# Reordering a convolution stage: three projection blocks ahead of the depthwise blocks, one joint LayerNorm tail, and squares and issues moved to GpSimd

**The chip, the cores, the metric.** The kernel runs on all 8 cores of one Trainium2 chip, each core with its own slice of the tokens. The metric is the device time of the slowest core in microseconds (us). Executions fall into two states: a fast one in which all cores show the same granted clock (the share of TensorE's full clock that the chip let through), and a slow one in which one die (or both) shows a lower clock and the time is some per cent longer, whatever the kernel. The five engines are called PE (TensorE, matmul), DVE (VectorE), ACT (ScalarE), POOL (GpSimd) and SP (SyncE, which here only starts transfers). In profile lines, `ps` is PSUM, the memory that PE writes its results to.

## The reference

Four layers, each a token mixer and a SwiGLU feed-forward network (FFN), each behind an RMS norm. Layers 1 and 3 use the mixer that this study is about:

```python
def conv_mixer(h, past, w_pw1, b_pw1, w_dw, b_dw, ln_g, ln_b, w_pw2, b_pw2):
    a = h @ w_pw1 + b_pw1                                   # pointwise-1: 1024 -> 2048
    glu = a[..., :D_MODEL] * jax.nn.sigmoid(a[..., D_MODEL:])
    padded = jnp.concatenate([past, glu], axis=1)
    new_state = padded[:, -CONV_STATE:]                     # last 30 rows, an output
    c = depthwise_conv(padded, w_dw, width=31) + b_dw       # one filter per channel
    c = jax.nn.silu(layer_norm(c, ln_g, ln_b))              # norm over the 1024 channels
    y = c @ w_pw2 + b_pw2                                   # pointwise-2: 1024 -> 1024
    return y, new_state
# in the trunk, per layer:  x = x + mixer(rms_norm(x));  x = x + swiglu(rms_norm(x))
```

## The kernel before

Channels lie on the 128 partitions, so 1024 channels are 8 blocks (`kc` 0 to 7). A core makes two passes over its tokens (`p` 0 and 1), with three token tiles in each (`tt`, widths 384, 384 and 256 in pass 0, up to 384, 384 and 320 in pass 1). A convolution stage therefore runs four times: two layers by two passes. I number them stages 1 to 4; 3 and 4 are pass 1.

A small scheduler records each operation with what it reads and writes and puts it on one engine's in-order queue; waits follow from the data. The depthwise convolution is done on PE: `stack` copies a pair of channel blocks four times, shifted, into a stacked buffer (16 transfers), and `dw` multiplies that with small 128x32 diagonal weights. The LayerNorm needs sums over channels, so a block's output is cast to bf16 and squared, and PE sums both with a matrix of ones.

```python
    def stat_a(kc, tt):                       # cast and square of one block, for the sums
        k_ = 2 * (len(slots) % 4)             # four shared slot pairs in SQ
        ...
        P.op("pool" if kc < 5 else "dve", ... tensor_copy(out=SQ[:, k_, 0:n], in_=CC.v[:, kc, c0:c0 + n]))
        P.op("act", ... activation(out=SQ[:, k_ + 1, 0:n], in_=CC.v[:, kc, c0:c0 + n], func=AF.Square))

    def stat_b(kc, tt): ...                   # PE adds both into two PSUM banks
    def ln_stats(tt): ...                     # mean and 1/std of one tile, in FT[0], FT[1]
    def ln_apply(tt):                         # scale 8 blocks, then 8 Silus, for one tile
        ...
                P.op("pool" if kc > 5 else "dve", ... tensor_tensor(CC, CC, FT[f], op))

    pw1(0); stack(0); build_w(0); build_w(1)
    pw1(1); stack(1)
    for kc in (0, 1):
        build_w(kc + 2)
        for tt in range(3): dw(kc, tt)
    pw1(2); stack(2)
    for kc in (2, 3):
        build_w(kc + 2)
        for tt in range(3): dw(kc, tt)
    pw1(3); stack(3, ("sp", "act"))
    load_p2(0); load_p2(1)                    # pointwise-2 weights, 1 MB each, on POOL's queue
    ...
    for tt in range(3):
        for kc in range(4): stat_a(kc, tt)
        dw(4, tt)
        for kc in range(4): stat_b(kc, tt)
    ...                                       # blocks 5 to 7 tile by tile, each tile's
    ...                                       # ln_stats and ln_apply between the next tile's blocks
    for tt in range(3):
        for m in range(KC):
            pw2(m, tt)                        # tile 2's statistics fall between these
            ...
                nnorm.square(k_, tt, *tb[tt]) # squares for the next RMS norm, on ACT
        nnorm.later(...)
```

## Time and profile before

| | kernel before |
|---|---|
| fast runs, all rounds of the study | 3903 to 3917 us, a few up to 3958 |
| profiled run (fast) | 3910.3 us, slowest core's span 3908.8 us |
| PE busy | 3633.7 us (93%) |
| span minus PE busy | 275 us, of which 156 us in the four convolution stages |
| table loads on ACT (instruction ACT_TABLE_LOAD) | 93 |

PE is the bound, so the profile is to be read for PE's idle time and for what ended it: the view of PE's waits gives the releaser, the timeline gives the place. Two readings are easily mixed up. A wait for a named tile ends when some engine or transfer has made it. A wait for "issue" is one in which nothing that the profile shows was missing.

### The profile page before, as it was taken

The page shows a single profiled execution, that of the slowest core. Times are in us where ns is not written, and L with a number is a line of the kernel's source. Part 1 is how long each engine was busy: PE and PEld are TensorE (multiplying, and loading weights), DVE is VectorE, ACT ScalarE, POOL GpSimd, SP SyncE. Part 2 cuts the span into 40 slices and gives each one's busy share as a digit, 9 for nine tenths or more (in the row PEclk, how much of TensorE's full clock was granted, in tenths as well). Part 3 has the DMA queues.
Part 4 walks back from the last instruction along what each step waited for, and adds up shares of the span by engine and source line. Part 5 has one row for each costly group of instructions (what it writes and reads, how often), then busy time and mean ns, then how long its engine had stood idle before and what let it go on. Part 6 is the DMA issues. An engine that isn't in the chain of part 4 may idle for free.

```text
span 3908.8 us, 71376 instructions; the slowest of 8 cores (3889.9 to 3908.8 us)
## 1 busy us (share of the span) xinstructions
PE 3633.7 (93%) x26325; PEld 2286.6 (59%) x26325; DVE 1710.2 (44%) x3324; ACT 1085.0 (28%) x2043; POOL 243.0 (6%) x376
## 2 busy tenths in 40 slices
PE   6999997899999999799599999879999999987998
PEld 2565664466466666466346666546664656654665
DVE  4875223521777213422377721334238772133422
ACT  3322112611432213521233211243124231124311
POOL 0000000100000000100001000020001000001000
PEclk9999998999999999899799999989999999998999
DMA  5443446244443445244534344544344434353433
GB/s 129 77 71 60 76 71 128 55 76 71 81 82 60 80 73 109 58 87 74 140 73 83 64 77 77 105 76 76 61 75 80 82 62 80 71 104 64 75 60 91
DMA packets 83807, 311.96 MB, mean 80 GB/s; under 512 B 14800, under 2 KB 27984, under 8 KB 66000
## 3 DMA queue, kind: packets, MB, share of 16 engines
q0 software_dynamic: 38016, 239.09, 34.8%
q1 hardware_dynamic: 42896, 63.75, 6.8%
q10 hardware_dynamic: 2560, 4.56, 0.6%
q8 instruction: 221, 3.62, 0.4%
q14 instruction: 114, 0.93, 0.1%
HBM read 499.23 MB, written 10.72 MB: 130 GB/s over the span
## 4 chain that ended last, share of the span: by engine, by line
PE 86%; DVE 4%; DMA 3%; issue 3%; ACT 2%; SPq 1%; ACTq 1%; DVEq 0%
PE ps L396 46%; PE ps L493 16%; PE ps L616 9%; PE ps L745 7%; PE ps L896 3%; PE ps L429 2%; DVE BIG L965 1%; SPq L880 1%; DMA xA<-xT 1%; DMA AUX<-BIG 1%; PE ps L701 1%; PE ps L391 1%; DVE xA L460 1%; ACTq L880 1%; DMA yT<-xA 1%
## 5 line engine op out<-in xcount | busy, mean ns | idle before, releaser
L396 PE MATMUL ps<-hA,RING 128*128 128x384 bf16 (+3 forms) x12672 | 1950.3, 314 | 2.7 <-issue 2.7
L396 PEld LDWEIGHTS ps<-hA,RING 128*128 128x128 bf16 x12672 | 1232.9, 98 | 640.9 <-issue 18.2
L485 DVE TENSOR_TENSOR BIG<-ps,FT 128x384 bf16<-128x384 f32 x528 | 276.1, 524 | 951.8 <-PE ps L396 906.9
L493 PE MATMUL ps<-BIG,RING 128*128 128x384 bf16 (+3 forms) x4224 | 634.0, 313 | 0.0
L493 PEld LDWEIGHTS ps<-BIG,RING 128*128 128x128 bf16 x4224 | 413.3, 98 | 217.4
L55 ACT ACTIVATE FT<-ps 128x384 f32<-128x384 f32 (+4 forms) x545 | 252.8, 465 | 968.9 <-PE ps L396 927.9
L460 DVE SCALAR_TENSOR_TENSOR xA<-ps,xA 128x384 f32<-128x384 f32 (+3 forms) x480 | 243.2, 522 | 567.4 <-PE ps L493 515.5
L55 ACT ACTIVATE SQ<-xA 128x384 bf16<-128x384 f32 (+3 forms) x432 | 188.9, 489 | 760.9 <-DVE xA L460 723.6
L745 PE MATMUL ps<-AUX,RING 128*128 128x384 bf16 (+3 forms) x2304 | 359.6, 312 | 21.6 <-DVE xA L460 21.2
L616 PE MATMUL ps<-RING,hA 128*128 128x512 bf16 x1584 | 345.3, 380 | 0.0
L745 PEld LDWEIGHTS ps<-AUX,RING 128*128 128x128 bf16 x2304 | 219.3, 98 | 140.0 <-issue 30.5
L616 PEld LDWEIGHTS ps<-RING,hA 128*128 128x128 bf16 x1584 | 155.2, 98 | 187.4 <-issue 2.2
L55 ACT ACTIVATE AUX<-ps,PPS 128x384 bf16<-128x384 f32 (+3 forms) x288 | 156.1, 557 | 362.8 <-PE ps L396 317.0
L445 DVE SCALAR_TENSOR_TENSOR hA<-xA,PPS,FT 128x384 bf16<-128x384 f32 (+3 forms) x384 | 194.3, 579 | 77.7 <-ACT FT L55 77.3
L713 DVE SCALAR_TENSOR_TENSOR FT<-ps,PPS,AUX 128x384 f32<-128x384 f32 (+1 forms) x288 | 163.7, 568 | 30.1 <-PE ps L701 23.0
L55 ACT ACTIVATE BIG<-ps 128x512 bf16<-128x512 f32 x198 | 118.1, 597 | 204.2 <-DVE ps L620 204.1
L729 DVE TENSOR_TENSOR AUX<-FT,AUX 128x384 bf16<-128x384 f32 (+3 forms) x288 | 151.3, 525 | 51.4 <-DVE FT L713 36.5
L620 DVE TENSOR_TENSOR ps<-ps,BV 128x512 f32<-128x512 f32 x210 | 145.9, 695 | 57.5 <-PE ps L616 55.8
L429 PE MATMUL ps<-SQ,ONESD 128*128 128x384 bf16 (+4 forms) x440 | 92.8, 326 | 83.8 <-ACT SQ L55 80.0
L832 DVE SCALAR_TENSOR_TENSOR BIG<-ps,PPS,FT 128x384 bf16<-128x384 f32 (+2 forms) x120 | 60.6, 508 | 235.2 <-PE ps L396 225.6
L53 ACT ACT_TABLE_LOAD x93 | 119.3, 1283 | 145.1 <-PE ps L429 41.6
L631 DVE BATCH_NORM_STATS2 STATS<-BIG 128x6 f32<-128x512 bf16 x198 | 135.4, 684 | 4.1 <-ACT BIG L55 3.9
(85 smaller groups left out, 1589.1 us busy)
## 6 DMA issues: line engine op xcount, KB each, us to landing
RING<-w_gu POOLq DMA_DIRECT2D x88, 1024.0 KB, 8.7
RING<-w_dn POOLq DMA_DIRECT2D x64, 704.0 KB, 6.6
RING<-w_v POOLq DMA_DIRECT2D x24, 1024.0 KB, 10.0
RING<-w_u POOLq DMA_DIRECT2D x32, 768.0 KB, 7.8
RING<-w_o POOLq DMA_DIRECT2D x32, 768.0 KB, 7.4
RING<-w_p POOLq DMA_DIRECT2D x24, 1024.0 KB, 10.5
AUX<-BIG SPq DMA_DIRECT2D x112, 147.0 KB, 8.5
AUX<-BIG SPq DMA_DIRECT2D x112, 131.5 KB, 8.7
```

The lines of the kernel that those rows point to most:

```text
L55: return self.e.activation(**kw)
L396: P.op("pe", [lambda e, kc=kc: e.matmul(ps[:, b, 0:n], lhsT=aps[kc], rhs=hA[:, kc, c0:c0 + n], start=(kc == 0), stop=(kc == KC - 1)) for k ...
L429: P.op("pe", lambda e, kc=kc: e.matmul(ps[:, b, 0:n], lhsT=ONESD[:, :], rhs=SQ[:, kc, 0:n], start=(kc == 0), stop=(kc == KC - 1)), reads=[ ...
L445: P.op("dve", lambda e, kc=kc, ap=ap, out=out: e.scalar_tensor_tensor(out=out, in0=ap, scalar=pcol(self.g, self.gi * KC + kc), in1=FT[:, f ...
L460: P.op("dve", lambda e: e.scalar_tensor_tensor(out=xA[:, m, c0:c0 + n], in0=ps[:, b, 0:n], scalar=bias, in1=xA[:, m, c0:c0 + n], op0=ALU.a ...
L485: P.op("dve", lambda e, bu=bu, n=n, f=f, mc=mc, c0=c0: e.tensor_tensor(out=A_.v[:, mc, c0:c0 + n], in0=ps[:, bu, 0:n], in1=FT[:, f, 0:n], ...
L493: P.op("pe", [lambda e, kc=kc: e.matmul(ps[:, b, 0:n], lhsT=w[:, kc, :], rhs=A_.v[:, kc, c0:c0 + n], start=(kc == 0), stop=(kc == 21)) for ...
L616: P.op("pe", [lambda e, kc=kc, b=b, cc0=cc0, wv=wv: e.matmul(ps[:, b, :], lhsT=hA[:, kc, cc0:cc0 + 128], rhs=wv[:, kc, :], start=(kc == 0) ...
L620: P.op("dve", lambda e, b=b, nb=nb: e.tensor_tensor(out=ps[:, b, :], in0=ps[:, b, :], in1=BV[:, nb % 2, :], op=ALU.add), reads=[("ps", b), ...
L713: P.op("dve", lambda e: e.scalar_tensor_tensor(out=FT[:, f, 0:nm].rearrange("p (a i) -> p a i", i=128), in0=ps[:, b, 0:nm].rearrange("p (a ...
L729: P.op("dve", lambda e: e.tensor_tensor(out=U.v[:, mc, c0:c0 + n], in0=FT[:, f, 0:n], in1=U.v[:, mc, c0:c0 + n], op=ALU.mult), reads=[("ft ...
L745: P.op("pe", [lambda e, kc=kc: e.matmul(ps[:, b, 0:n], lhsT=w[:, kc, off:off + 128], rhs=U.v[:, kc, c0:c0 + n], start=(kc == 0), stop=(kc ...
```

## The change

The intent: hide the stack copies behind PE work, take the sums' inputs off the path, and join the LayerNorm tails.

1. Convolution blocks 0 to 3 all run after three pointwise-1 blocks; before, blocks 0 and 1 ran after two.
2. Casts and squares of blocks 0 to 2 are made during pointwise-1 block 4, in slots of their own; the copy queue on ACT goes to POOL.
3. The LayerNorm tail treats the tiles jointly, with statistics of their own and four table loads fewer a stage; POOL scales blocks 1 and 4.
4. Half of the next norm's squares go to POOL, and the first FFN weight load (`gu_load`, 1 MB) is issued before block 5 instead of at the start of the FFN.

```diff
-            pw1(0)
-            stack(0)
-            ...                      (the order shown above)
+            for m2 in range(3):
+                pw1(m2)
+                if m2 < 2:
+                    stack(m2)
+                    build_w(2 * m2)
+                    build_w(2 * m2 + 1)
+            for kc in range(4):
+                for tt in range(3):
+                    dw(kc, tt)
+                if kc < 2:
+                    build_w(kc + 4)
+                if kc == 1:
+                    stack(2)
+            pw1(3, [lambda s=s: load_p2(s) for s in range(2)]
+                + [lambda kc=kc, tt=tt: stat_a(kc, tt) for kc in range(3) for tt in range(3)])
+            stack(3, ("sp", "pool", "sp"))
             build_w(6)
             build_w(7)
+            for tt in range(3):
+                stat_a(3, tt)
...
             for tt in range(3):
-                for kc in range(4):
-                    stat_a(kc, tt)
                 dw(4, tt)
                 for kc in range(4):
                     stat_b(kc, tt)
+                stat_a(4, tt)
+            gu_load(2 * l + 1, 0)
...                                   (joint tail: blocks 6 and 7 of all tiles, then)
+                P.op("pool" if kc in (1, 4) else "dve", ... tensor_tensor(CC, CC, f_, op))   # scale
...
-                        nnorm.square(k_, tt, *tb[tt])
+                        nnorm.square(k_, tt, *tb[tt], pool=(k_ % 2 == 0))
```

(The whole tail is cut; its order is told where it matters. Two small moves are cut too: the copy of the running stream's tail in pass 0, and the order in which the first pointwise-2 group reads its blocks.)

## The prediction

> **What bounds the kernel now.** I read first the page's shares of busy time, then the waits of the matmul engine (PE), then its timeline in the four places where the changed code runs, then busy time, clock and DMA in stretches of 2 us, then ACT and DVE in the tail of such a stage. I take every figure from the fast state: the profiled run was one (3910.3 us, all cores near clock 0.972). The other three runs of before (4066 to 4509 us) were slower than the 1.5% rule allows for fast ones.
>
> The page says that PE sets the time:
>
> ```profile
> PE 3633.7 (93%) x26325; PEld 2286.6 (59%) x26325; DVE 1710.2 (44%) x3324; ACT 1085.0 (28%) x2043; POOL 243.0 (6%) x376
> ```
>
> So the change can win only where PE stands still: 3908.8 - 3633.7 = 275 us. PE's waits say for what (line, releaser, us in total, times, longest):
>
> ```profile
> PE ps L429 <- ACT SQ L55: 80.0, 11, 34.3
> PE ps L939 <- DVE SQ L922: 50.9, 8, 8.0
> PE ps L939 <- ACT SQ L55: 43.3, 12, 8.6
> PE ps L896 <- DMA AUX<-BIG: 37.3, 4, 13.4
> ```
>
> The first is almost all the load of x at the two starts and stays. The other three, 131.5 us, are the convolution stage: L896 is the depthwise convolution waiting for its stacked copy, L939 the LayerNorm sums waiting for casts (L922) and squares. It runs four times. Its stretches from the end of the second pointwise block to the end of the last one, with PE busy and the mean clock:
>
> ```profile
> 610.40:757.30 146.90, 106.64 (x1218) 65.66 (x1218) 59.58 (x113) 66.01 (x121) 23.32 (x31) 0.86 0.42 84
> 1524.80:1663.10 138.30, 106.11 (x1217) 66.07 (x1218) 56.56 (x103) 65.86 (x121) 23.35 (x31) 0.89 0.40 78
> 2509.30:2665.80 156.50, 114.85 (x1473) 70.92 (x1474) 62.55 (x119) 67.64 (x121) 22.84 (x31) 0.86 0.46 85
> 3486.90:3646.10 159.20, 117.58 (x1473) 71.99 (x1474) 63.58 (x124) 67.69 (x121) 23.42 (x31) 0.85 0.42 79
> ```
>
> Span minus PE busy is 156 us over the four. That is not all that is lost: 14% of the clock is missing there too. In the first stage:
>
> ```profile
> 623.77 8.43 PE L896 MATMUL ps<-AUX 128*32 128x384 bf16 x177 [13.35 <-DMA AUX<-BIG]
> 634.21 0.62 PE L896 MATMUL ps<-AUX 128*32 128x256 bf16 x15 [2.01 <-issue]
> ...
> 649.18 7.13 PE L896 MATMUL ps<-AUX,BV 128*32 128x384 bf16 x192
> ...
> 679.67 2.40 PE L939 MATMUL ps<-SQ,ONESD 128*128 128x384 bf16 x7 [7.25 <-ACT SQ L55]
> ...
> 711.25 0.80 PE L939 MATMUL ps<-SQ,ONESD 128*128 128x384 bf16 x2 [7.86 <-DVE SQ L922]
> ...
> 726.92 0.59 PE L939 MATMUL ps<-SQ,ONESD 128*128 128x256 bf16 x2 [5.00 <-DVE SQ L922]
> ```
>
> After the wait of 13.35 us, 177 matmuls take 8.43 us, where 192 take 7.13 us without one. At full speed the work of the first stretch is: two pointwise-1 blocks 28.8 (14.4 each, 656.25 to 670.67), eight channel blocks of convolution 28.3 (7.07 for two), sums 8.4, pointwise-2 27.8 and the next norm's sums 2.6, in all 96 us. So about 51 of 146.9 us are lost. The same sum for the others (96, 101 and 102 us of work) gives 42, 55 and 57: 205 us in all, 5.2% of the span. This is the ceiling of the change. By cause: 37 idle for the stack copy, 31 for the first sums, 67 in the tail, 18 "issue", 3 small, and some 45 to 50 of slow matmuls after them.
>
> **What the Trainium skill says.**
> - "TensorE: Matmul & The Clock Gate", section "What's actually happening": the array clock halves after about one idle window (3.4 us) and comes back after about as long a busy one. The trace agrees: granted clock 0.50 from 615 to 627 us, with PE at work again from 623.8.
> - "DMA: Bandwidth & Descriptors", sections "Queues, rings and completion order" and "Issuing engines are not separate DMA queues": queues share the same 16 DMA engines and take turns, and another issuing engine saves issue time only. The trace agrees: stack copies and weight loads together stay near 200 GB/s at a share of about 1.0 until 632 us:
>
> ```profile
> 629.00:631.00 2.00, 2.00 (x56) 1.36 (x51) 0.00 (x0) 1.16 (x3) 0.00 (x0) 1.00 1.08 198
> 631.00:633.00 2.00, 1.20 (x37) 0.76 (x25) 0.00 (x0) 0.65 (x2) 0.00 (x0) 1.00 0.48 92
> ```
>
> - "ScalarE: Activation LUTs", section "What ACT_TABLE_LOAD costs": some 1283 ns for a table load. The trace has 1283 ns for all 93, 7 of them in one such stretch.
> - "GPSIMD Engine Reference", section "4.1 Engine selection": two-input elementwise work is about 2x slower there. The trace has 998 against 552 ns (medians of L965).
>
> **The change, part by part.** The matmuls stay the same in number and shape; only order, buffers and engines move. Each sum is for one stage unless said.
>
> *1. Convolution blocks 0 to 3 run after three pointwise blocks, not two.* The 14.4 us of the third block now lie under the first stack copy. In stage 1, PE reaches the convolution at 610.4 + 14.4 = 624.8, and the copy had landed by 623.8; the others have more room (their waits were 6.9, 7.1 and 9.9). So the 37 us go, and some 10 of slow clock with them. But blocks 2 and 3 now follow at once, 7.1 us later (7.9 in pass 1), and need the second copy. Before, DMA was busy until about 632.0, 1544.1, 2530.5 and 3510.2. To this comes the second pointwise-2 load, issued when the third pointwise block ends (at 649.8 before, near 625.3 now). One copy's packets take 11.1 us of all 16 engines (queues 1 and 10 held 42.3% of 105 us for four), one load 6.3 (18% of 105 for three). If they share, the copy lands near 638.3 against a need at 631.9; with the same sum in the other stages I get new waits of 6.4, 1.4, 5.2 and 6.9, together 20, plus 4 for the clock. Net gain 47 - 24 = 23.
>
> *2. "Issue" gaps, 18 us.* They come 70 to 180 matmuls into a convolution burst while DMA is saturated. The burst is now twice as long and still under saturated DMA. I keep two thirds, because part falls inside the wait of part 1: gain 6.
>
> *3. Casts and squares of blocks 0 to 2 move into pointwise block 4, with slots of their own for every block and tile.* The wait of about 7.7 us before the first sums goes (31 idle, 10 slow). It came from 8 stack DMAs on ACT (672.0 to 679.0) ahead of the squares; those go to POOL. In return the last copy is closer. Say pointwise block 4 ends at T. The copy starts at T + 1.3 and landed at about T + 13.4 before (684 against 670.7). PE has until block 6 only 7.1 (blocks 4, 5) + 3.6 + 1.2 (sums) = 11.9 us of work. POOL also issues five copies before the casts of block 3, so those sums wait about 2.4 us. The early FFN load starts moving near T + 12 and delays the copy's rest to about T + 15. So 3.5 us stay lost: 41 - 14 = 27 gained over the four.
>
> *4. The LayerNorm tail.* Let 0 be the start of block 6, tile 0. ACT: sums of tile 0 reach it at 5.9; copy, square, DVE's subtraction, table load and root (0.57 + 0.6 + 0.65 + 1.28 + 0.61) end at 9.65. Only then comes block 7's tile 1 eviction, at 9.5 to 10.1 (they overlap), because ACT goes in order. DVE: cast at 10.3, two blocks' scaling at 4 x 0.62, a cast, one block, a cast at 15.0, the subtraction of tile 1, three blocks at 6 x 0.62 to 19.2, the subtraction of tile 2. ACT: root of tile 2 at 20.4, Silu table 21.7, eight Silus at 0.62: 26.7. PE's first pointwise-2 group ends at 26.9 and PE has 11.9 us of work until then. Loss 15 plus about 2 of clock, against 22.5 a stage before (67 idle + 23 slow). After that nothing stops PE: DVE needs 1.44 us per group for an add and two 256-wide scalings (0.58 + 2 x 0.43) beside PE's 1.31, with all eight PSUM banks free. Net gain 4 x 5.5 = 22.
>
> *5. The rest.* Four table loads fewer a stage (93 to 77), half of the squares to POOL, the FFN load earlier: PE showed no wait for those, so 0.
>
> Sum: 23 + 6 + 27 + 22 = 78 us. I take off 4 for small new collisions: 74 us, so 3910 - 74 = 3836 us, 1.9%. The four stretches should fall from 601 to about 527.
>
> **Rivals.**
> *The copies are hidden.* The stack copies go ahead of the loads, or the loads start late. For it: packets of a copy are many and queued early. Against it: loads landed in 9.8 to 13.4 us beside copies, against 6.3 of work, so they get more than half. Then the waits of parts 1 and 3 nearly vanish: 24 + 10 more, 3800 us.
> *DMA becomes the bound.* Copies, loads and instruction fetches pile up in a shorter stretch and the gaps return as waits for AUX<-BIG and "issue". For it: each stage's four copies and four loads are 4 x 11.1 + 4 x 6.3 = 70 us of DMA and PE would pass them in about 130. Then parts 1 to 3 give half: 3865 us.
> *The tail stays as long.* One tile-wide chain of three tiles' statistics before the first Silu is longer than before's per-tile chains; DVE at 0.69 instead of 0.62 (as in one stretch where POOL worked too) adds 1 to 2 us a stage. Then part 4 gives nothing: 3858 us.
> *A slowdown* needs all of part 1 and 3 lost and the tail longer by 6 us a stage; I see no sign of it.
>
> **Range and chances.** The sum's terms are uncertain by about 12 each for parts 1 to 3 and 15 for the tail, together some 25. From 3836 that gives 3802 to 3868 for 8 in 10, in the fast state. The 2% line is at 3910 / 1.02 = 3833 us, beside my value, so it is nearly even: faster 0.46, same 0.52, slower 0.02. A median that mixes in slow runs lies higher and isn't meant.
>
> **What would show it.** Right: no wait for AUX<-BIG at the first convolution block, one of 1 to 7 us 192 matmuls later (256 in pass 1); no 7 us gap before the first sums; one gap of some 10 us before the first pointwise-2 group with DVE scaling under it; 77 table loads. Wrong: PE waits for the copy at blocks 0 or 6 by over 5 us; sums waiting on POOL; waits inside pointwise-2, which would mean that DVE and POOL can't keep pace with the third tile; a clock below 0.97 on all cores because PE idles less, which no line of before suggests.

## More of the kernel before

The page's list of transfer queues has one line whose meaning I passed over at first:

```profile
q8 instruction: 221, 3.62, 0.4%
```

(Queue and kind; packets, MB, share of the 16 DMA engines' time.) By its kind, queue 8 moves no data of the kernel: its 221 packets of 3.62 MB / 221 = 16.4 KB each are instructions, and they take time of the same 16 DMA engines. (Queue 14 is of the same kind, with 114 smaller packets.)

## The result

Fast runs of the kernel after took 3851.9 to 3859.0 us. The ratio of the fast runs is 0.9859 with a 95% interval of 0.9844 to 0.9874: 1.4% less time. Every ratio here is from the fast runs of both kernels in the same rounds, so it is not quite the ratio of any two times quoted. The profiled run of after was fast (3851.0 us, all clocks 0.977 to 0.979).

The page of the kernel after:

```profile
PE 3622.7 (94%) x26325; PEld 2277.7 (59%) x26325; DVE 1729.5 (45%) x3330; ACT 1045.1 (27%) x1979; POOL 292.5 (8%) x444
```

PE's waits after (line, releaser, us in total, times, longest). L916 and L922 are the depthwise convolution, L962 the LayerNorm sums, L390 a first group of a pointwise or FFN matmul:

```profile
PE ps L390 <- ACT hA L54: 34.6, 4, 8.9
PE ps L916 <- issue: 25.1, 10, 4.8
...
PE ps L962 <- DVE SQ L947: 15.6, 4, 4.2
PE ps L962 <- POOL BIG L947: 11.9, 4, 3.4
PE ps L922 <- issue: 4.4, 4, 3.1
PE ps L962 <- DVE BIG L947: 4.1, 6, 0.8
...
PE ps L916 <- DMA AUX<-BIG: 1.8, 2, 1.5
```

The three waits that carried the prediction have gone or shrunk: 37.3 us for the stack copy became 1.8, 43.3 us for ACT's squares vanished, and 50.9 for DVE's casts became 19.7 (15.6 + 4.1; some casts now go to a buffer of another name). In their place stand 34.6 us for the normalized tile ahead of pointwise-2, 11.9 for POOL's casts and 29.5 (25.1 + 4.4) of "issue".

The four stretches of after, with the same ends as those of before (window; us; busy PE, PEld, DVE, ACT and POOL; clock; DMA share; GB/s):

```profile
610.40:737.90 127.50, 102.77 (x1218) 63.56 (x1216) 64.25 (x115) 57.22 (x107) 33.20 (x45) 0.92 0.45 92
1521.60:1648.30 126.70, 103.19 (x1171) 63.84 (x1164) 64.93 (x113) 61.45 (x113) 34.05 (x48) 0.91 0.38 74
2474.60:2615.30 140.70, 113.39 (x1477) 68.69 (x1475) 64.77 (x117) 59.50 (x109) 34.45 (x45) 0.87 0.56 100
3439.40:3586.20 146.80, 116.78 (x1474) 69.47 (x1472) 68.02 (x123) 58.80 (x107) 34.11 (x45) 0.87 0.49 82
```

They are 19.4, 11.6, 15.8 and 12.4 us shorter, 59.2 in all, and the spans differ by 3908.8 - 3849.5 = 59.3: the whole change in time lies there. Predicted was 601 to 527; it is 541.7.

Stage 1 on PE shows the new shape (start, us, tile, count, and in brackets the idle time before and what ended it):

```profile
624.04 3.11 PE L916 MATMUL ps<-AUX 128*32 128x384 bf16 x76
630.52 4.20 PE L916 MATMUL ps<-AUX 128*32 128x256 bf16 x116 [3.36 <-issue]
...
637.10 6.80 PE L916 MATMUL ps<-AUX,BV 128*32 128x384 bf16 x183 [1.90 <-issue]
...
663.95 0.48 PE L962 MATMUL ps<-BIG,ONESD 128*128 128x384 bf16 x2 [3.12 <-POOL BIG L947]
...
701.42 3.47 PE L390 MATMUL ps<-hA,RING 128*128 128x384 bf16 x6 [8.76 <-ACT hA L54]
```

The first convolution block starts without a wait, at 624.04. The burst is broken twice by "issue", the sums wait once for POOL, and pointwise-2 starts at 701.42, 27.3 us after block 6 (674.15).

Let T be the end of pointwise-1 block 4. I use three lengths below: A, from the first convolution matmul to the start of that block (at full pace 14.1 us in pass 0 and 15.8 in pass 1, 59.8 over the four stages); L, from T to the end of the last convolution matmul; and S, from T to the start of pointwise-2.

| kernel after | stage 1 | 2 | 3 | 4 |
|---|---|---|---|---|
| A | 19.8 | 20.9 | 22.5 | 23.1 |
| L | 27.2 | 26.1 | 38.8 | 41.8 |
| S | 43.2 | 42.1 | 53.4 | 56.6 |

Pass 1 has more columns, but that is worth only a few us: best values of L seen there later are near 30 to 34. So some 8 us a stage are lost in the tail of pass 1 alone. The table is of the slowest core. All eight were traced: over them L in after is 34.6 to 41.6 us in stage 3 and 38.5 to 43.4 in stage 4, so one core alone decides nothing smaller than a few us.

### The profile page after: what moved, and what is told of

Same layout as the page of the kernel before. It is cut to its first block, busy times and chain, and to the rows that moved or that the text cites. A ratio compares the mean times of both kernels' runs of the same rounds, so it can differ in the third digit from the quotient of the medians.

```text
span 3849.5 us, 71399 instructions; the slowest of 8 cores (3832.4 to 3849.5 us)
## 1 busy us (share of the span) xinstructions
PE 3622.7 (94%) x26325; PEld 2277.7 (59%) x26325; DVE 1729.5 (45%) x3330; ACT 1045.1 (27%) x1979; POOL 292.5 (8%) x444
## 4 chain that ended last, share of the span: by engine, by line
PE 89%; DVE 3%; DMA 3%; issue 2%; ACT 1%; SPq 1%; POOL 0%; DVEq 0%; ACTq 0%; POOLq 0%
PE ps L395 48%; PE ps L503 16%; PE ps L626 9%; PE ps L755 8%; PE ps L916 3%; PE ps L432 2%; PE ps L390 1%; DMA yT<-xA 1%; PE ps L711 1%; DMA xA<-xT 1%; DVE BIG L994 1%; DMA AUX<-BIG 1%; DVE xA L463 1%; PE ps L962 1%; PE ps L621 1%
## 5 line engine op out<-in xcount | busy, mean ns | idle before, releaser
L54 ACT ACTIVATE SQ<-xA 128x384 bf16<-128x384 f32 (+3 forms) x384 | 169.3, 489 | 778.4 <-DVE xA L463 740.4
L54 ACT ACTIVATE BIG<-ps 128x512 bf16<-128x512 f32 (+1 forms) x202 | 119.5, 593 | 200.9 <-DVE ps L630 200.8
L630 DVE TENSOR_TENSOR ps<-ps,BV 128x512 f32<-128x512 f32 x210 | 145.6, 694 | 53.4 <-PE ps L626 52.7
L348 POOL DMA_DIRECT2D RING<-w_gu x88 | 46.9, 533 | 1107.7 <-PE ps L395 885.6
```

The lines of the kernel that those rows point to most:

```text
L54: return self.e.activation(**kw)
L630: P.op("dve", lambda e, b=b, nb=nb: e.tensor_tensor(out=ps[:, b, :], in0=ps[:, b, :], in1=BV[:, nb % 2, :], op=ALU.add), reads=[("ps", b), ...
```

## The experiments

Eighteen kernels ran, all with correct results. Each was timed in five rounds against the kernel before. Unless said otherwise, figures of a trace are of the slowest core of one profiled execution. Where e2, e8, e9, e11, e16 and e17 are concerned, read e18 as well: a part of them, the late state writes, did not do what I thought.

### e5_order_only: only the first part of the change

```diff
 kernel before, with one change: the order of part 1
+  pw1 0, 1, 2 first, then dw 0 to 3, with stack(2) after block 1
```

> The kernel before with one part of the change alone: three pointwise-1 blocks, then convolution blocks 0 to 3, then the fourth; buffers, casts, tail and loads as before. Theory (this part gave 38.7 of the change's 59 us, as the stretches from the first convolution to the fourth pointwise block say): 3910 minus 35 to 42, ratio 0.989 to 0.991; no wait for AUX<-BIG at block 0, issue gaps of 3 to 5 us in the burst. Rival (the stretch only passes its loss to what follows, because the last copy and the squares behind ACT's DMA issues set the time): the wait before the first sums grows by as much, ratio 0.995 or more.

Measured: 3867.9 to 3871.7 us, ratio 0.9894 (0.9879 to 0.9908), 41 us less than before. The order alone carries over two thirds of the gain. Its A sums to 87.9 us, like after's 86.3, so the other parts add nothing to A. It had one long wait for the second copy, of 7.4 us, in the one stage where no "issue" gap came first: the copy landed at 640 us in stage 1, against 638 worked out, and where PE had already stood still for "issue", that wait is simply hidden under it.

### e1_scale_dve: LayerNorm scaling without POOL

```diff
-                    P.op("pool" if kc in (1, 4) else "dve", ...   # scale
+                    P.op("dve", ...
```

> The changed kernel with the LayerNorm scaling of blocks 1 and 4 moved from POOL to DVE, nothing else. Theory (DVE is slowed by POOL working beside it): in the tail DVE took 4.54 us for 4 and 6.01 us for 6 scalings beside POOL, 7.39 us for 12 mostly alone. So 16 alone take about 9.5 us where 12 took 11.8, the first pointwise-2 group of each stage starts about 25 us instead of 27.2 us after block 6 starts, DVE's mean for these instructions falls to about 0.6 us in the tail, and the time falls by 5 to 8 us: ratio to before 0.984 to 0.985. Rival (the length of the chain is the number of DVE instructions in it): 4 more of them at 0.9 us each put that group 3 to 4 us later, 31 us, ratio 0.989 to 0.990.

Measured: 3845.0 to 3847.8 us; the ratio 0.9809 has a wide interval (0.9754 to 0.9863) because two of before's runs were at 3936 and 3958. That is some 9 us less than after's fast runs, which were of other rounds. The instructions of the scaling line, first after, then e1 (count; ns min/median/max):

```profile
L994 DVE TENSOR_TENSOR BIG<-BIG,FT x96: 541/559/1357, 685.8 to 3552.4; 128x384 f32<-128x384 f32 x96
...
L994 POOL TENSOR_TENSOR BIG<-BIG,FT x32: 992/1123/1308, 681.2 to 3542.4; 128x384 f32<-128x384 f32 x32
```

```profile
L994 DVE TENSOR_TENSOR BIG<-BIG,FT x128: 548/556/559, 687.3 to 3549.5; 128x384 f32<-128x384 f32 x128
```

Without POOL beside it, none of 128 scalings took over 559 ns; beside it some took up to 1357. The theory's ratio of 0.984 to 0.985 lies in e1's interval, the rival's 0.989 to 0.990 outside it. The DVE timeline in stage 1 shows which scalings were slow, in after:

```profile
685.85 4.54 DVE L994 TENSOR_TENSOR BIG<-BIG,FT 128x384 f32<-128x384 f32 x4
...
690.51 1.21 DVE L994 TENSOR_TENSOR BIG<-BIG,FT 128x384 f32<-128x384 f32 x2
...
692.31 6.01 DVE L994 TENSOR_TENSOR BIG<-BIG,FT 128x384 f32<-128x384 f32 x6
```

and POOL's own in after, at the same time:

```profile
684.71 4.60 POOL L994 TENSOR_TENSOR BIG<-BIG,FT 128x384 f32<-128x384 f32 x4 [2.55 <-ACT FT L54]
...
693.25 3.66 POOL L994 TENSOR_TENSOR BIG<-BIG,FT 128x384 f32<-128x384 f32 x3 [3.93 <-ACT FT L54]
```

One by one, the scalings that DVE ran wholly beside POOL's took 1.16 to 1.35 us in these lines, whereas the two between the groups (690.51), with POOL idle, took 0.56 each, and so did the last of the first group, which began when POOL had finished. POOL's own took 1.11 to 1.31 us beside DVE, and 0.99 alone. From 693.44 to 697.43 three DVE scalings started 1.33 us apart on average, each beside one of POOL's. The Trainium skill, "SBUF — State Buffer", section "SBUF: two separate sides", says that a VectorE instruction with two SBUF inputs and a GpSimd instruction that reads SBUF exclude each other by a lock for a whole instruction. The trace agrees in kind. It does not agree in full: full exclusion would cost 0.56 + 0.99 = 1.55 us a pair, and a pair took some 1.33 (the profile's times for POOL are rough). The wait ahead of pointwise-2 fell from 34.6 to 25.4 us, but S only by 1.2 us a stage in pass 0, since DVE now has four scalings more in tile 0.

### e2_late_state: state writes behind pointwise-2 (a test that tested nothing)

```diff
-            if p == 1:
-                P.dma("sp", ... convT[...] <- CST ...)      # two transfers, right behind stack(3)
...
+            if p == 1:                                       # the same two, behind the pw2 loops
+                P.dma("sp", ...)
```

> The changed kernel with the two writes of the new convolution state (pass 1 only) issued after pointwise-2 instead of right after the last stack copy, nothing else. Theory (these writes of 120-byte pieces keep the DMA engines busy at 25 to 60 GB/s and hold up PE's instructions): the issue gaps in blocks 4 to 7 of pass 1 (0.2 and 4.8 us in stage 3, 0.3, 2.5 and 4.0 us in stage 4) shrink to under 1 us together, with some 3 us of slow matmuls: minus 12 to 15 us, ratio 0.982 to 0.983. Rival (the early FFN weight load holds them up): the gaps stay, ratio within 0.001 of the changed kernel's 0.9859.

Measured: 3849.7 to 3854.3 us, ratio 0.9828 (0.9763 to 0.9893), same as after; the gaps in the tail of pass 1 stayed (6.0 us in stage 4, 3.8 in stage 3). I first took this as the end of the theory that the state writes cause them. It was not: the trace shows the writes issued at 2542.3 us, against 2539.7 in after. SP has nothing else in its queue and the data had been ready, so a later place in the program moved nothing.

### e3_gu_late and e14_no_pool_sq: the early FFN load, and what it repays

```diff
 e3:  -            gu_load(2 * l + 1, 0)
 e14: -            gu_load(2 * l + 1, 0)
      -                        nnorm.square(k_, tt, *tb[tt], pool=(k_ % 2 == 0))
      +                        nnorm.square(k_, tt, *tb[tt])
```

> The changed kernel with the first FFN weight load back at the start of the FFN, nothing else. Theory of the state writes: the issue gaps of pass 1 shrink by a third at most (the writes still fill the engines), pass 0 is unchanged: minus 0 to 5 us, ratio 0.9847 to 0.986. Rival (the load is what holds PE up): the gaps of blocks 4 to 7 go, ratio 0.982 to 0.983. If the early load was worth something, PE waits for w_gu at the start of the FFN and the ratio is above 0.986.

e3 measured: 3894.1 to 3898.5 us, ratio 0.9935 (0.9892 to 0.9978), 41 us more than after. PE's waits in e3, one new line:

```profile
PE ps L390 <- DMA RING<-w_gu: 52.0, 4, 13.9
```

and POOL's timeline there says why:

```profile
744.60 0.61 POOL L423 TENSOR_TENSOR SQ<-xA 128x256 bf16<-128x256 f32 x1 [0.17 <-POOL SQ L423]
745.16 1.69 POOL L348 DMA_DIRECT2D RING<-w_gu  x3
```

POOL is in-order. The change had put the squares of the next norm on it, so a load issued "at the start of the FFN" now stands behind the last square. That was one reading; e14 takes the squares off POOL as well:

> e3_gu_late (no early FFN load) with the next norm's squares all back on ScalarE. Theory (e3's 52 us of waits for the FFN weights come from the load standing behind the squares in POOL's in-order queue): the load is issued some 20 us before its use again, the waits for w_gu vanish, and the time is that of the kernel after or a little less, 3840 to 3852 us, ratio 0.982 to 0.986. Rival (the FFN load was late for other reasons, such as ring space or the DMA engines): the waits of about 13 us per stage stay, 3885 to 3900 us, 0.993 to 0.997. A third way: squares on ScalarE alone come late and the next norm's sums wait for them, 1 to 3 us a stage.

e14 measured: 3838.8 to 3842.4 us, ratio 0.9820 (0.9805 to 0.9836). No wait for `w_gu` is left, so POOL's queue was the cause. And without both, squares on POOL and early load, the kernel is some 14 us faster than after: the pair is a net loss. Its L in stages 3 and 4 is 33.0 and 35.1 us instead of 38.8 and 41.8, so what the early load costs is paid in the tail of pass 1.

### e6_gu_mid: the early load a little later

```diff
-            gu_load(2 * l + 1, 0)            # before block 5
...
             for kc in range(3):
                 scale(0, kc)
+            gu_load(2 * l + 1, 0)            # behind POOL's first scaling
```

> The changed kernel with the early FFN weight load issued by POOL after its first scaling of tile 0 (some 25 us after pointwise block 4) instead of after the casts of block 4 (some 11 us), nothing else. Theory (this load, beside the last copy, holds up PE's instructions in pass 1, and the early place is needed only because POOL's squares would otherwise stand before it): the gaps of blocks 4 to 7 in pass 1 fall from 11.6 us to about 3 us as in the run without the early load, and no wait for w_gu comes at the FFN: minus 10 to 15 us, ratio 0.982 to 0.983. Rival (the gaps are those of the state writes): no change, 0.985 to 0.986.

Measured: 3839.6 to 3843.2 us, ratio 0.9820 (0.9805 to 0.9834), as the theory said. L in stages 3 and 4 fell to 32.0 and 33.0 us. Nothing about the load has changed except when it is under way.

### e4_cast_first: POOL's casts of block 3 ahead of the last copy

```diff
+            for tt in range(3):
+                stat_a(3, tt)
             stack(3, ("sp", "pool", "sp"))
             build_w(6)
             build_w(7)
-            for tt in range(3):
-                stat_a(3, tt)
```

> The changed kernel with the casts and squares of block 3 put ahead of the last stack copy, nothing else. Theory (the sums wait because POOL first issues five copies, 2.7 us): the four waits for POOL of 3.1, 2.3, 3.0 and 3.4 us go, the copy starts at most 2 us later and has that room: minus 9 to 13 us with the slow matmuls that follow the wait in stages 3 and 4, ratio 0.9825 to 0.9835. Rival (the last copy is as tight): block 6 waits for AUX<-BIG by 2 to 3 us in each stage instead, ratio 0.985 to 0.986.

Measured: 3857.2 to 3862.9 us and one run at 3911.7, ratio 0.9872 (0.9805 to 0.9940). The rival held, with longer waits than its 2 to 3 us. The wait of 11.9 us for POOL's casts is gone, and in its place e4 has among PE's waits:

```profile
PE ps L916 <- DMA AUX<-BIG: 41.5, 6, 11.9
```

Block 6 now waits 7.3, 4.6, 11.9 and 10.9 us for the last copy: POOL issues its share of that copy later, and the FFN load is issued (668.37) while the copy is still being issued.

### e7_tail, e8_all, e9_sum_late: a different tail

e7 makes all three tiles' sums first, splits the root off, puts all casts on POOL and all scaling on DVE. e8 is e7 with block 3's casts first, the FFN load behind block 7's casts and the (ineffective) late state writes. e9 is e8 with the next norm's sums later.

```diff
 e7, tail, in the new order
+            dw(6, 1); stat_a(6, 1); stat_b(7, 0); stat_b(5, 1); ln_var(0)
+            dw(7, 1); stat_a(7, 1); stat_b(6, 1); ln_root(0)
+            dw(6, 2); ...; scale(0, 0); dw(7, 2); ...; ln_var(1); ...
+            for kc in range(1, 4): scale(0, kc)
+            ln_root(1); ln_var(2); ln_root(2)
+            for kc in range(4, KC): scale(0, kc)
 e9
-                nnorm.later(tt, *tb[tt], 2 if tt < 2 else 1, 1)
+                nnorm.later(tt, *tb[tt], (5, 3, 1)[tt], 1)
```

> The changed kernel with another tail: all sums of the three tiles before most of the scaling, the root of each tile split from its variance so that ACT does not wait between, all casts on POOL, all scaling on DVE. Theory (what holds the first pointwise-2 group is one in-order chain on DVE, slowed by POOL): the first group ends 22 to 24 us after block 6 starts instead of 32, minus 30 to 36 us over four stages, ratio 0.977 to 0.979, if pass 1's gaps stay. Rival (the chain is only moved: PE then waits for tile 1's Silus or for a free bank): minus 5 to 15 us, 0.982 to 0.9845, with waits for ACT hA at tile 1.

e7 measured: 3857.6 to 3869.7 us, ratio 0.9878 (0.9858 to 0.9898), some 8 us slower than after and outside both expectations. The rival was right that the chain only moves, but not where to. Pointwise-2 started 21.6 us after block 6 instead of 27.3, but DVE then carried 24 scalings of the later tiles in a row (13.7 us), and the residual adds and squares of pointwise-2 stood behind them: the next norm's sums waited some 4 us a stage.

> The new tail, the FFN load behind the casts of block 7, the casts of block 3 before the last copy, and the state writes after pointwise-2. Theory (the three costs are separate): minus 33 (tail), 12 (load), 9 (casts, which wait for POOL 11.9 us in the changed kernel and made the copy late only because the load stood beside it): 3850 to about 3797, ratio 0.970 to 0.973. Rival (the last copy is the floor under block 6 whatever comes before): waits for AUX<-BIG at block 6 of 2 us or more in each stage, 0.975 to 0.978.

e8 measured: 3841.1 to 3846.9 us, ratio 0.9827 (0.9810 to 0.9843); its profile fell in the slow state, and on the undisturbed die block 6 waited for the last copy 2.0, 4.9 and 3.2 us in stages 1, 3 and 4 (core 2). That is 47 us above the theory and above the rival too: the three gains do not add up.

> e8_all with the next norm's row sums issued later in the next block, so that they no longer come before the squares they need. Theory (the short waits for squares of 0.5 to 1.5 us each at the start of the next norm are pure loss, 3 to 4 us per stage): these waits go, 12 to 16 us off e8_all, about 3826 us, ratio to before 0.978 to 0.980. Rival (VectorE's backlog of scalings is the floor, the stall only moves to the next banks): no change, 0.982 to 0.984, with the waits for VectorE or ScalarE elsewhere grown by as much.

e9 measured: 3848.8 to 3851.1 us and one run at 3889.6, ratio 0.9872 (0.9817 to 0.9926), a little slower than e8. The short waits for ACT's squares went (91.7 us on e8's core 2, 82.4 in e9, with the start-up included), but waits for POOL's squares rose from 9.3 to 26.2 us, up to 4.8 us each. The rival held here too: the stall moved.

### e10_p2_late, e11_both, e12_p2_after_copy, e13_p2_block4: one pair of loads, four places

The two pointwise-2 loads (1 MB each) start with the first convolution burst in after. These kernels are built on e6 and only move those loads; e11 is e9 with e10's move.

```diff
 e10: -   pw1(3, [load_p2(0), load_p2(1)] + [stat_a ...])
      +   pw1(3, [stat_a ...] + [load_p2(0), load_p2(1)])     # behind the casts of blocks 0 to 2
 e12:     ... not in pw1(3), but behind stat_a(3, ...), and so behind the last copy's issues
 e13:     ... not there, but behind stat_a(4, ...), when the last copy should have landed
```

> e6_gu_mid with the two pointwise-2 weight loads issued behind the casts, so that they are not under way in the first burst of convolution blocks. Theory (the pauses in TensorE's first burst and the waits for the second stack copy come from the DMA engines being full): the loss from the first convolution matmul to the fourth pointwise-1 block falls from about 26 us to about 10 over the four stages, 12 to 20 us off e6_gu_mid, 3822 to 3830 us, ratio 0.977 to 0.979. Rival (the pauses come from the rate of TensorE's instructions in the burst or from the stack copies alone): no change, 0.981 to 0.983.

e10 measured: 3834.7 to 3839.6 us, ratio 0.9814 (0.9797 to 0.9832). Half of the theory held. A fell from 85.2 us (e6) to 69.0, the 16 us that were expected, but S grew from 182.7 to 195.3, and PE waited 7.2 and 5.6 us for a copy in stages 1 and 2. The gaps of the first burst come from the loads; moved, the loads delay the next copy. I took that copy for the last one. It is the third: the wait stands before block 4, right behind pointwise-1 block 4 (653.57 to 660.76 us in stage 1), because the loads were issued at 636.96, in the midst of the third copy's transfers. The expectation of e12 repeats this mistake.

> e9_sum_late and the late pointwise-2 loads together. If both theories hold the gains add: 3805 to 3815 us, ratio 0.973 to 0.976. If only one holds, as that one alone, 0.978 to 0.980; if neither, 0.982.

e11 measured: 3842.9 to 3846.1 us, ratio 0.9832 (0.9814 to 0.9849): of the two theories neither adds up, as e9 and e10 had shown.

> e10_p2_late with the two pointwise-2 loads issued one step later, behind block 3's casts and so behind the last stack copy's issues. In e10 the first burst lost 16 us less than in e6_gu_mid but block 6 then waited 7.2 and 5.6 us for the last copy in stages 1 and 2, the loads and that copy being under way together, while the DMA engines lie idle from about 672 to 695 us. Theory (a load under way beside a stack copy is what costs, in either place): both gains are kept, TensorE waits for the last copy under 1 us per stage, 8 to 13 us off e10, 3823 to 3829 us, ratio to before 0.978 to 0.980. Rival (the wait only moves: the loads meet the FFN load behind POOL's first scaling, and pointwise-2 waits for its weights, or block 3's sums wait for POOL again): 0.981 to 0.983.

e12 measured: 3863.7 to 3867.4 us, ratio 0.9887 (0.9869 to 0.9905), the worst of the four and outside both expectations. A was 62.9 us, but among PE's waits of e12 there is:

```profile
PE ps L916 <- DMA AUX<-BIG: 36.1, 4, 13.1
```

Being issued behind the copy does not put a load behind it. Now it is the last copy that was still under way, and block 6 waited 8.3, 7.5, 13.1 and 7.1 us for it.

> e12_p2_after_copy with the two pointwise-2 loads issued behind POOL's casts of block 4, about 8 us later, when the last stack copy should have landed. Theory (loads beside copies cost): TensorE's waits for the last copy fall from 7 to 13 us a stage to under 1 us, the loss in the first burst stays as small as in e10 and e12 (first convolution matmul to fourth pointwise-1 block 63 to 69 us over four stages instead of 85), and the loads still land before pointwise-2: 3822 to 3830 us, ratio to before 0.977 to 0.980. Rival (the wait for the last copy in e12 comes from the copy being issued closer behind the faster burst, not from the loads): 5 us or more of wait stays in each stage, 3850 to 3865 us, 0.985 to 0.989.

e13 measured: 3835.8 to 3839.7 us, ratio 0.9814 (0.9797 to 0.9832). The waits for any copy are gone, in all four stages, and A stayed small (15.6, 15.6, 16.7, 18.6), so the loads beside the copies were the cause of both, as the theory said. The time is not as low as expected because L in stages 3 and 4 rose to 40.5 and 42.9 us, with "issue" gaps of 6.7 and 7.2 us in them. Whatever was under way in the tail of pass 1 now met the pointwise-2 loads.

### e15_best: e13 with DVE scaling tile 0 alone

```diff
-  casts of block 5 on DVE; scale: "pool" if kc in (1, 4)
+  casts of block 5 on POOL; scale: "pool" if kc in (1, 4) and tt; FFN load behind block 5's casts
```

> e13_p2_block4 with tile 0's LayerNorm scaling all on VectorE, block 5's casts on POOL in exchange and the FFN load behind those casts. Theory (VectorE and POOL slow each other in tile 0's scaling, about 4 to 5 us a stage, and POOL is idle at block 5): the wait before the first pointwise-2 group falls from 8.8 to about 6 us, 8 to 14 us off e13, 3812 to 3820 us, ratio 0.975 to 0.977. Rivals: the FFN load now meets the pointwise-2 loads and they come late, a wait for weights in pointwise-2; or VectorE's longer list in tile 0 eats the gain: as e13.

Measured: 3838.2 to 3840.6 us, ratio 0.9818 (0.9803 to 0.9834): no gain over e13, the last rival. Tile 0's first six scalings took 4.08 us instead of 4.54 for four, but tile 1's six still took 6.01, now beside POOL's, and the wait ahead of pointwise-2 stayed (8.8 us in pass 0, 9.6 and 10.2 in pass 1).

### e16_joined, e17_joined_dve, e18_state_act: what is under way in the tail of pass 1

e16 is e14 (no squares on POOL, no early FFN load) with e13's place for the pointwise-2 loads and e2's state writes; e17 adds e15's scaling to it.

```diff
 e18, against e16
-                P.dma("sp", ... convT[...] <- CST ...)       # behind the pw2 loops, on SP
+                P.dma("act", ... convT[...] <- CST ...)      # the same place, on ACT's in-order queue
```

> e14_no_pool_sq (no early FFN load, squares on ScalarE) with the pointwise-2 loads behind block 4's casts as in e13 and the state writes after pointwise-2 as in e2. Theory (the pauses in the tail of pass 1 appear where transfers are under way): the first burst's stretch falls from 84.6 to about 66 us over four stages as in e13, the time from the end of the fourth pointwise-1 block to the last convolution in stages 3 and 4 stays near 33 us instead of 40 and 43, so 14 to 20 us off e14: 3820 to 3827 us, ratio to before 0.977 to 0.979. Rival (the pauses come with the longer stream of small matmuls in pass 1, whatever DMA does): 40 us and more stay there, 3832 to 3840 us, 0.981 to 0.983.

e16 measured: 3832.5 and 3834.7 us, and a third fast run at 3885.0 that widens the ratio to 0.9869 (0.9809 to 0.9928). A fell as expected, to 65.5 us. L stayed at 38.8 and 44.0 us, as the rival had it. But the rival's reason was not shown, since e16's timeline of SP in stage 3 reveals e2's mistake:

```profile
2499.48 28.37 SPq L900 DMA_DIRECT2D AUX<-BIG  x19
2527.89 1.19 SPq L1097 DMA_DIRECT2D convT<-CST  x1
```

The state write (L1097) is issued the moment the last copy has been issued, at 2527.9 us, though the program has it behind pointwise-2, which ran from 2566. PE's gaps of e16 in that stretch:

```profile
2547.19 1.54 PE L916 MATMUL ps<-AUX,BV 128*32 128x384 bf16 x44 [2.00 <-issue]
...
2554.05 0.30 PE L922 MATMUL ps<-AUX,BV 128*32 128x64 bf16 x16 [3.27 <-issue]
```

> e16_joined with tile 0's scaling all on VectorE and block 5's casts on POOL. Theory (contention costs 4 to 5 us a stage): pointwise-2 starts about 2 to 3 us earlier after the fourth pointwise-1 block in each stage, 8 to 12 us off e16, 3810 to 3818 us, ratio 0.975 to 0.977. Rival (as in e15, where the wait for ScalarE's normalized tile stayed 8.8 us: the four more scalings on VectorE cost what the missing contention saves): no change against e16.

e17 measured: 3836.3 to 3840.6 us, ratio 0.9814 (0.9800 to 0.9827): the rival again, no change against e16.

> e16_joined with the state writes issued by ScalarE instead of SP, at the end of the stage. Theory (the small packets of the state writes fill the DMA engines and hold up what TensorE needs to go on): in stages 3 and 4 the time from the end of the fourth pointwise-1 block to the last convolution falls from 38.8 and 44.0 us to 30 to 34, the pauses without a releaser in the tails from some 7 and 12 us to under 3 each, 12 to 18 us off e16: 3814 to 3822 us, ratio to before 0.975 to 0.978. Rival (the pauses come from pass 1's longer stream of matmuls, or from the pointwise-2 loads alone): the two stretches stay at 37 us and more, no change against e16's undisturbed runs of 3832 to 3835, 0.980 to 0.982. A third way: the writes now slow pointwise-2 instead (pauses there), the same total.

e18 measured: 3817.7 and 3824.1 us, ratio 0.9771 (0.9743 to 0.9799), the only kernel whose whole interval lies below 0.98. Only two of its eight runs were fast, and its profile fell in the slow state; its die 0 was undisturbed, with spans of 3808 to 3819 us, against 3826 to 3831 for all cores of e16. I read its lines on core 3, of that die. The theory of e18 held. The writes were issued late:

```profile
L1097 ACTq DMA_DIRECT2D convT<-CST x2: 378/402/427, 2605.1 to 3556.5; - x2
```

and the view of the transfers between 2528 and 2560 us shows what left with them. First e16, then e18 (DMA: busy tenths of the 16 engines in 40 slices; GB/s in the same slices):

```profile
DMA  8795999978999249485997985999998200000000
GB/s 197 131 120 89 78 57 37 66 13 21 64 42 41 10 31 92 51 113 82 184 215 123 174 92 102 195 184 184 174 236 174 51 0 0 0 20 0 0 0 0
DMA packets 2556, 2.76 MB, mean 86 GB/s; under 512 B 2153, under 2 KB 2153, under 8 KB 2294
```

```profile
DMA  9999899976999999997000000000000000000000
...
DMA packets 625, 2.79 MB, mean 87 GB/s; under 512 B 105, under 2 KB 105, under 8 KB 363
```

The same 2.8 MB took until about 2554 in e16 and until 2543 in e18. In e16 the engines are busy at 10 to 120 GB/s for half of that time, with 2153 packets under 512 B: the state writes carry only 240 KB, and with them under way the engines were done some 10 us later. The pointwise-2 loads landed after 20.4 us in e16 and 12.9 in e18. L in stages 3 and 4 became 34.5 and 32.1 us, and all "issue" gaps of the convolution together 6.7 us (after: 29.5). The two fast runs do not stand alone: over all eight cores of the profiles, L in stages 3 and 4 is 37.4 to 44.1 and 41.4 to 46.4 us in e16, and 29.8 to 35.0 and 31.8 to 33.4 in e18. The edit changed two things, the time of the writes and their queue; no run separates them, but the packet counts show what was under way. e18 joins what held, and it beats both the kernel before and the kernel after.

**What "issue" is.** The Trainium skill, "Runtime: NRT & Kernel Launch", section "Instruction fetch mechanics", says that an engine's instruction memory is refilled in blocks of 16 KiB (256 instructions) over a DMA queue, and calls the cost "mostly hidden". The trace has 221 such packets of 16.4 KB. One block is 128 matmuls with their weight loads, and a convolution burst eats one in about 4.7 us (128 of 192 matmuls in 7.1 us). In each of the four gaps that I looked at closely (e16's two above and the two of stage 1 in after) exactly one instruction packet was moved within about 1 us of the gap's start, and no other in the gap. In e18, with no gap in stage 1's burst, four packets came at 626, 630, 635 and 640 us. So a burst starved of instructions by full DMA engines explains the gaps, their place, and why moving transfers moves them.

The packed traces say more than these four. Over all twenty kernels and eight cores, PE has 802 "issue" pauses of 1 us or more in the depthwise matmuls, and 86% of them end 1.2 to 1.8 us after a packet of queue 8 has finished (median 1.46 us). The same holds for 9% of 9600 of these matmuls picked at random from those without a pause, for 6% of 800 waits of other kinds, and, with packets of queue 14 instead, for 3% of the pauses. The size fits as well: 26325 matmuls and as many weight loads are 206 blocks of 256, and queue 8 moved 221 packets. So what ends most of these pauses is the arrival of a block of PE's instructions. That full DMA engines are what makes the block late is supported by every run that moved a transfer, and not shown by itself: no run changed the fetching alone.

| kernel | lowest fast time, us | ratio to before |
|---|---|---|
| after | 3851.9 | 0.9859 |
| e5, order only | 3867.9 | 0.9894 |
| e1, scaling on DVE | 3845.0 | 0.9809 (wide) |
| e3, no early FFN load | 3894.1 | 0.9935 |
| e6, FFN load later | 3839.6 | 0.9820 |
| e14, squares on ACT, no early load | 3838.8 | 0.9820 |
| e13, e6 with pointwise-2 loads behind block 4 | 3835.8 | 0.9814 |
| e16, e14 with those loads behind block 4 | 3832.5 | 0.9869 (wide) |
| e18, e16 with state writes on ACT's queue | 3817.7 | 0.9771 |

## Why the prediction was right or wrong

The time of the fast runs, 3852 to 3859 us, lies inside the range, the likeliest class (within 2%) came out, and no slowdown. The value was 3836, so about 20 us of the expected 74 did not come. Two steps failed, in distinct terms of the sum: part 4's price for the scalings on DVE (twelve at 0.62 us, 7.4 us; they took 11.8), and part 3's account of the early FFN load in pass 1 (a delay of the last copy alone; it cost PE about 15 us in pauses and slow matmuls). The path and the waits that the prediction named were otherwise the right ones.

**Parts 1 and 2, the first burst (29 expected).** Measured in the profiles, the loss from PE's readiness for the first convolution block to pointwise-1 block 4, less the work, fell from 65.2 to 26.5 us: 38.7 gained. e5 alone gained 41. The mechanism of part 1 was right: the first copy is hidden, the second lands near 640 us in stage 1 (e5). Its division was wrong. The second copy's wait of 20 us became 1.8, and instead 17.5 us of "issue" came, which I had meant to shrink to 12 over the whole stage; the two overlap in time (e5), so I should not have charged them both. e13 and e18 show how much was there: A within 1 to 7 us of pure work.

**Part 3, casts and squares early (27 expected).** The wait for the sums went as said, and POOL's wait is what I worked out: 3.12, 2.29, 3.04 and 3.40 us against 2.4 a stage. In pass 0, block 6 started 15.9 and 15.1 us after T, against 15 predicted, but that is luck: the prediction has the last copy landing then, and PE did not wait for the copy at all. The 11.9 us of work and POOL's wait of 3.12 and 2.29 us fill most of the time. In pass 1 the step fails, by about 15 us (L of 38.8 and 41.8 against 32.0 and 33.0 in e6, 34.5 and 32.1 in e18): "the early FFN load ... delays the copy's rest to about T + 15" took a transfer's cost to be the copy's delay only. PE lost 5.3 and 6.8 us to "issue" there, and more to slow matmuls behind the gaps (the granted clock was 0.50 from 2552 to 2556 us). e6 shows the load's part, by moving it. The load met the state writes, which the prediction does not mention at all. Their part is shown by e18 only beside the pointwise-2 loads; beside the FFN load no run moved them, since e2 did not.

**Part 4, the tail (22 expected).** The chain was the right one, link by link, and the size of one link was wrong. The twelve scalings of tile 0 on DVE took 4.54 + 1.21 + 6.01 = 11.8 us for 7.4, because POOL worked beside them (e1). So the Silu table load came at 25.1 us after block 6 instead of 20.4, and the first pointwise-2 group ended near 32 instead of 26.9: close to 5 us a stage, 19 in all, nearly the whole 22. The rival "the tail stays as long" named this cause and sized it at 1 to 2 us a stage. The evidence was in the profile of before, in the scaling line whose maximum was 1355 ns beside a median of 552; my 0.62 us was near the median. e1, e15 and e17 show further that the loss is not simply to be had back: without POOL, DVE has 16 scalings for 12, and S fell by only 1.2 us a stage in pass 0.

**Part 5, the rest (0 expected).** The 77 table loads came as said. But "so 0" hides two terms of opposite sign: squares on POOL cost some 55 us if the FFN load stays at its place (e3 against e14), and the early load buys back 41 of them (after against e3); together they lose some 14 us (after against e14). This is the loss of part 3 in pass 1 seen from another side, and not a further one. I had looked for waits of PE for those operations in the profile of before and found none, which says only that there was nothing to gain. Moving work to an idle engine also puts it ahead of what that engine already issues.

**The sum and the rivals.** Tail and pass 1 missed by about 19 + 15 = 34 us, the first burst came out 10 better than its 29, and 4 had been set aside; 74 - 34 + 10 + 4 leaves 54, near the 55 that the ratio gives (3910 x 0.0141). The errors have both signs, so that the time lies only 20 us above the value is partly luck. The rival that came truest is "the tail stays as long", 3858 us: 19 of part 4's 22 us did not come. "DMA becomes the bound", 3865 us, expected parts 1 to 3 to give half of their 56 us, and by this account they gave about 51; but it named the "issue" gaps, which returned.

**What stays open.** What delays the instruction blocks, tested by itself; how DVE and POOL share their access so that a pair takes some 1.33 us and not 0.99 or 1.55; what the state writes cost beside the FFN load in after; and how e18 would do with more than two fast runs.

## What to carry to other kernels

Ask of each transfer that a change moves what else is under way at that moment, small packets above all: the same two loads made 27 us of difference between e12 and e13, issued seven microseconds apart; and an operation issued "later" on an idle queue is issued at once. An idle engine is not a free one: before work goes to it, look at what it issues (POOL's loads) and with whom it shares memory access (DVE), and look in the profile for the longest duration where two of them will run together, not for the median. After an experiment that moves something, check in its trace that it did move.

## What the Trainium skill lacked or had wrong

- "Runtime: NRT & Kernel Launch", section "Instruction fetch mechanics", calls the refill of instructions mostly hidden. Here PE's pauses without a releaser reached 8.3 us in one place (e1) and 29.5 us in the convolution stages of one execution of after while the DMA engines were full, and 6.7 us when three groups of transfers had been moved elsewhere. 86% of 802 such pauses in all traces ended 1.2 to 1.8 us after an instruction packet had finished. That a stream of short matmuls can wait for its instructions in this way is not on the page; that full DMA engines cause it is supported and not proven.
- "SBUF — State Buffer", section "SBUF: two separate sides", has the rule that the shared access of VectorE and GpSimd is an exclusive lock, but no duration for two-input work on both. Here a 128x384 f32 two-input instruction on DVE went from 0.56 us to between 1.16 and 1.35 with POOL at the same kind of work, and POOL's from 0.99 to between 1.11 and 1.31. A pair took some 1.33 us, less than the 1.55 that full exclusion would give.
- "GPSIMD Engine Reference", section "4.1 Engine selection", compares the engines alone (2x; here 0.99 against 0.56 us). That is no measure of what splitting the work brings: a pair of one instruction on each took some 1.33 us, and two on DVE alone 1.11 us.
- "DMA: Bandwidth & Descriptors", section "Issuing engines are not separate DMA queues": agreed, and what small packets cost the large transfers that they mix with is missing. With 240 KB of writes in over 2000 packets under 512 B beside them, two 1 MB loads landed after 20.4 us instead of 12.9 (e16, e18), and with two such loads issued behind a stack copy PE waited 7 to 13 us for that copy (e12).
- I found no page that says that a transfer's place in the program means nothing on an idle issuing queue. Here a write placed behind some 40 us of work was issued at 2542.3 us instead of 2539.7.
